# The seam between attention and the MLP: first W1 blocks and x operands asked for during the last value product

## The chip, the cores and the metric

One core of a Trainium2 chip runs one program. The metric is the device time of one execution in microseconds (us), the median of several runs. The engines have queues of their own: TensorE (PE, with its weight loads PEld), VectorE (DVE), ScalarE (ACT), GpSimd (POOL), and SyncE (SP), which here issues nearly all transfers.

## The reference

One bidirectional encoder layer over 2048 positions of width 1024, in float32. The change touches the seam between its last two parts:

```python
    h = h + _cross_attention(_rms_norm(h, norm_x_g[l]), _rms_norm(mem, norm_mem_g[l]),
                             xa_wq[l], xa_wk[l], xa_wv[l], xa_wo[l])
    h = h + jnp.square(jax.nn.relu(_rms_norm(h, norm_ff_g[l]) @ ff_w1[l])) @ ff_w2[l]
return _rms_norm(h, final_norm_g)
```

Ahead of it stand a mixer (a long convolution beside an mLSTM) and its output projection. `ff_w1` is 1024 x 4096, `ff_w2` 4096 x 1024, `mem` has 256 tokens and four heads.

## The kernel before, in words

Activations are kept transposed, channels on the 128 partitions, in blocks of 128 x 512 (256 KB). Every float32 product is made of three: each operand is split into a high half (a rounding copy on ScalarE, line 1539 or 1569) and a low half (a subtraction on VectorE or GpSimd, line 1540 or 1570), and `mm3` (lines 340 to 342) adds high x high, high x low and low x high into one PSUM bank.

**Attention.** `attention` works through four chunks of 512 positions, c = 0 to 3. Each has eight products for the mixer's output projection, the scores with their softmax (tiles `e`, four of them), and eight value products ct = 0 to 7 (24 matmuls each), into which the output weights have been folded. After each value product `finish` adds the residual into a block of `acc`, squares it and adds to the row sum `ssum` (GpSimd, line 1389); `store` writes the block times the norm's gain to `hg` and, after ct = 3 and 7, four residual blocks to `h2` (line 1490, 1 MB). `stats` turns the row sum into the mean square and stores it (line 1518).

**The MLP.** It treats both products as 2 x 2 blocks and makes each with seven block products instead of eight, with sums and differences of blocks. `tp` is the half of the positions, `g` one of 16 groups of 256 hidden channels. `steps` walks (tp, g, i) with i in `ORDER_UP` = 1, 2, 6, 7, 5, 4, 3; the first two groups go side by side, so steps n = 0 and 1 are i = 1 for g = 0 and 1, steps 2 and 3 are i = 2, steps 4 and 5 are i = 6. Each step is one `ffn_product` of 12 matmuls. Its operands:

- x operand i (`ffn_xload` asks for four blocks, `ffn_x` splits them). Operands 1, 2 and 3 are blocks of `hg`; 5, 6, 7 and 4 are sums that `sums_x` has made on GpSimd and stored in `xs`. Four `sums_x` sets for tp = 0 are written into chunk 2's value products.
- weight operand: `load_w1(g)` asks for four W1 blocks (line 1586), makes two sums on GpSimd (lines 1589 and 1590) and, for g below 4, saves them to DRAM for the second half (`save_w1`, line 1577). `ffn_w1` makes the rest of the sums (lines 1611 and 1615) and splits one into `ah`, `al`.

`ffn_pre` fetches x operands 1, 2 and 6 and the weights of the first four steps during chunk 3's value products. In `ffn` the loop asks for W1 of group n at n = 0 and 1, and for x operands 7, 5, 4, 3 at n = 0, 2, 4, 6. Between the value products and this loop stand the first two products and `stats`.

**What sets the order.** The program is written as if in sequence; a planner with a timeline of its own (`schedule_with_timeline_sim`) then fixes the order of each engine's queue, and may take an instruction ahead of others when its data and its buffers are ready. Tiles of one tag share `bufs` buffers in turn: `wr` (6) holds blocks of x and W1 on arrival and also the last mean `mb`; `w` (12) the W1 blocks, in a pool `wring` opened in `ffn`, after attention's pool is closed; `sm` (4) the blocks of `sums_x`; `act`, `wh`, `wl` operands of products. In the up phase the blocks of `acc` serve as scratch, taken in turn from block 1:

```python
def tmp():
    turns[0] += 1
    return self.acc[:, turns[0] % 8]
```

Of the kernel before, what the change touches and what calls it, by code (L numbers as in the profile page):

```python
# [133 lines left out]
class Prog:  # L134
# [1173 lines left out]
    def attention(self, es):  # L1308
        nc, tc, a = self.nc, self.tc, self.a
# [25 lines left out]
        def gemm(w, i, r, p=None, ks=range(8)):  # L1335
            p = p or self.mm()
            ms = slice(128 * i, 128 * i + 128)
            for k in ks:
                self.mm3(p, w[0][:, k, ms], w[1][:, k, ms], r[0][:, k], r[1][:, k], k == 0, k == 7)
            return p  # L1340
# [32 lines left out]
        for c in range(4):  # L1373
# [7 lines left out]
            def finish(ct, p, ssum):  # L1381
                h = acc[:, ct]
                nc.vector.tensor_tensor(h, p, h, ALU.add)
                if ct == 0:
                    nc.scalar.activation(ssum, h, AF.Square)
                else:
                    sq = A.tile([128, 512], F32, tag="sq", name="sq", bufs=1)
                    nc.scalar.activation(sq, h, AF.Square)  # L1388
                    nc.gpsimd.tensor_tensor(ssum, ssum, sq, ALU.add)  # L1389
# [3 lines left out]
            for ct in range(8):  # L1393
                yield 5.2
                if ct % 2 == 0:
                    w = next(wst)
                else:
                    k = sums.pop(0) if sums else None
                    if k is not None:
                        self.sums_x(A, k, "sm")  # L1400
                if c == 0 and ct == 0:
                    half = [gemm(w, i, y, None, range(4)) for i in range(2)]
                    next(mix)
                    residual(0)
                    residual(1)
                if c == 0 and ct < 2:
                    p = gemm(w, ct, y, half[ct], range(4, 8))
                else:
                    p = gemm(w, ct % 2, y)
                if c > 0 and ct < 2:  # L1410
                    residual(ct)
                if ct == 0 and stats is not None:
                    stats()
                if prev is not None:
                    finish(ct - 1, prev, ssum)
                    self.split_gain(s[0][:, ct - 1], s[1][:, ct - 1], acc[:, ct - 1], gx[:, ct - 1:ct])
                prev = p
# [64 lines left out]
            ssum = A.tile([128, 512], F32, tag="ssum", name="ssum", bufs=2)  # L1482
            prev = None

            def store(ct):
                hg = A.tile([128, 512], F32, tag="hg", name="hg", bufs=2)
                nc.scalar.activation(hg, acc[:, ct], AF.Copy, scale=gf[:, ct:ct + 1])
                nc.scalar.dma_start(out=hgd[c, :, ct], in_=hg)
                if ct % 4 == 3:
                    nc.sync.dma_start(out=h2[c, :, ct - 3:ct + 1], in_=acc[:, ct - 3:ct + 1])  # L1490

            for ct in range(8):
                yield 5.2
                if ct % 2 == 0:
                    w = next(wst) if ct else w
                else:
                    k = sums.pop(0) if sums else None
                    if k is not None:
                        self.sums_x(A, k, "sm")
                if c == 3 and ct in (1, 3, 5):  # L1500
                    self.ffn_pre(ct // 2)
                p = gemm(w, ct, o, half[ct], range(4, 8)) if ct < 2 else gemm(w, ct % 2, o)
                if prev is not None:
                    finish(ct - 1, prev, ssum)
                    store(ct - 1)
                prev = p
            finish(7, prev, ssum)
            store(7)

            def stats(c=c, ssum=ssum):  # L1510
                pr = self.hy()
                nc.tensor.matmul(pr, self.ones, ssum, start=True, stop=True)
                if c < 3:
                    mb = A.tile([128, 512], F32, tag="sq", name="mb", bufs=1)
                else:
                    mb = self.R.tile([128, 512], F32, tag="wr", name="mb", bufs=6)
                nc.vector.tensor_scalar(mb, pr, 1.0 / D, EPS, ALU.mult, ALU.add)
                nc.sync.dma_start(out=msd[c], in_=mb)
                pr = self.hy()
                for t in range(4):  # L1520
                    nc.tensor.matmul(pr[:, t:t + 1], ssum[:, 128 * t:128 * t + 128], self.ones[:, 0:1], start=True, stop=True)
                nc.vector.tensor_scalar(rbp[:, 4 * c:4 * c + 4], pr[:, 0:4], 1.0 / D, EPS, ALU.mult, ALU.add)
                nc.vector.scalar_tensor_tensor(rbp[:, 4 * c:4 * c + 4], rbp[:, 4 * c:4 * c + 4], EPS,
                                               rbp[:, 4 * c:4 * c + 4], ALU.mult, ALU.mult)
        self.first = [self.ffn_product(self.wq.pop(0), 1) for _ in range(2)]
        stats()

    ORDER_UP = (1, 2, 6, 7, 5, 4, 3)
    ORDER_DOWN = (1, 6, 7, 5, 3, 2, 4)
# [13 lines left out]
    def ffn_open(self, es):  # L1543
        es.enter_context(self.tc.tile_pool(name="even", bufs=1, side="right")).tile([128, 120], F32, name="even")
        self.R = es.enter_context(self.tc.tile_pool(name="ring", bufs=1, side="right"))
        self.xt, self.rs = {}, es
        self.W, self.WD = {}, {}

    def ffn_xload(self, tp, i):
        hg = self.dram("hg", (4, 128, 8, 512))  # L1550
# [23 lines left out]
        return self.C.tile([128, 512], F32, tag="w", name="w", bufs=12)  # L1574

    def save_w1(self, g, j, t):
        self.nc.sync.dma_start(out=self.dram("w1s", (4, 4, 128, 512))[g, j], in_=t)

    def load_w1(self, g):
        op = self.nc.gpsimd.tensor_tensor  # L1580
# [62 lines left out]
    def ffn(self):  # L1643
# [2 lines left out]
        groups = [(0, (0, 1))] + [(0, (g,)) for g in range(2, 14)] + [(0, (14, 15)), (1, (0, 1))]  # L1646
        groups += [(1, (g,)) for g in range(2, 16)]
        steps = [(tp, g, i) for tp, gs in groups for i in self.ORDER_UP for g in gs]
        self.C = self.rs.enter_context(tc.tile_pool(name="wring", bufs=1, side="right"))
        prods = [(o, i) for o in range(4) for i in self.ORDER_DOWN]  # L1650
        down = [(n, tp, k) for n in range(len(prods)) for tp in range(2) for k in range(4)]
        aq, bq = {}, {}
# [32 lines left out]
        with tc.tile_pool(name="up", bufs=1) as U:  # L1685
# [24 lines left out]
            xsum = list(range(4, 8))  # L1710
            us, cs = {}, {}
            for n, (tp, g, i) in enumerate(steps):
                if n < 2:
                    self.load_w1(n)
                if n < 8 and n % 2 == 0:
                    j = self.ORDER_UP[n // 2 + 3]
                    self.ffn_x(j, self.ffn_xload(0, j))
                if n + 5 < len(steps) and steps[n + 5][0] and steps[n + 5][1] < 4:
                    self.saved.append(self.ffn_w1_saved(*steps[n + 5][1:]))
                if 4 <= n + 2 < len(steps):  # L1720
                    wq.append(self.ffn_w1(*steps[n + 2]))
                if n + 9 >= len(steps) and n + 5 < len(steps):
                    load_w(0, n + 9 - len(steps))
                if n + 2 >= len(steps):
                    k = n + 2 - len(steps)
                    fetch_b(k)
                    fetch_a(0, k)
                if i == 4 and xsum and g % 2 and 2 < g < 13:
                    self.sums_x(self.T, xsum.pop(0), "wn")
                bank = self.ffn_product(wq.pop(0), i) if n > 1 else self.first[n]  # L1730
                u, c = us.setdefault(g, {}), cs.setdefault(g, {})
                if i == 1:
                    u[1] = tmp()
                    nc.scalar.copy(u[1], bank)
                elif i == 2:
                    c[11] = fin(bank, u[1], tp, g, 1)
                elif i == 6:
                    u[2] = plus(bank, u[1])
                elif i == 7:
                    u[3] = plus(bank, u[2])  # L1740
                elif i == 5:
                    c[22] = fin(bank, u[3], tp, g, 3)
                    u[4] = plus(bank, u[2])
                elif i == 4:
                    c[21] = fin(bank, u[3], tp, g, 2)
                else:
                    c[12] = fin(bank, u[4], tp, g, 0)
                    if n + 1 == len(steps):
                        fetch_a(0, 2)
                        fetch_b(2)  # L1750
                        fetch_a(0, 3)
                    t = [self.stage() for _ in range(4)]
                    op = nc.gpsimd.tensor_tensor
                    op(t[0], c[12], c[11], ALU.subtract)
                    op(t[1], c[22], t[0], ALU.subtract)
                    op(t[2], c[22], c[12], ALU.subtract)
                    op(t[3], c[21], t[1], ALU.subtract)
                    for j, x in zip((5, 6, 7, 4), t):
                        out(tp, g, j, x)
                if g == 15 and tp == 0:  # L1760
                    self.ffn_x(i, self.ffn_xload(1, i))
# [241 lines left out]
```

## Time and profile before

| | before |
|---|---|
| median of 3 runs | 3198.08 us |
| the runs | 3193.67, 3198.08, 3198.31 us |
| the profiled execution | 3195.44 us |
| its span, first to last instruction | 3193.7 us |
| mean granted TensorE clock | 0.978 |
| TensorE busy | 96% of the span |
| VectorE, ScalarE, GpSimd busy | 64%, 47%, 36% |
| memory read and written | 404.15 MB, 202.41 MB |

Times in the trace are microseconds from the start of the span. Chunk 3's value products run to about 1909, the up phase begins there. A line number is that of the kernel before. A row of a timeline has start, length, engine, line, operation, output and inputs, count, and in brackets how long the engine had stood idle before it and for whom.

### The profile page before, as it was taken

How to read it: one execution, taken by the hardware profiler on the slowest of the kernel's cores; microseconds unless marked ns; L12 is line 12 of the kernel's file. 1: busy time of each engine (PE TensorE's matmuls, PEld its weight loads, DVE VectorE, ACT ScalarE, POOL GpSimd, SP SyncE). 2: the span in 40 equal slices, each digit the busy share in tenths (PEclk: the TensorE clock that was granted, in tenths of full speed). 3: DMA queues.
4: the chain of work that ended last, by engine and by line, in shares of the span. 5: the costliest groups of instructions: out<-in, count | busy, mean ns of one | idle time of the engine just before them, and what ended most of it. 6: DMA issues, size and time to landing. Idle time of an engine off the chain costs nothing.

```text
span 3193.7 us, 43601 instructions
## 1 busy us (share of the span) xinstructions
PE 3050.3 (96%) x14473; PEld 2399.5 (75%) x14473; DVE 2056.9 (64%) x3563; ACT 1503.6 (47%) x2873; POOL 1156.5 (36%) x802
## 2 busy tenths in 40 slices
PE   6999999999999977999999998999999999999998
PEld 4655566776668766888887886888888878888876
DVE  7775366444874767877775556566655676655695
ACT  5543366424764344454544445556555443333335
POOL 0122012100121334324151217776566483434483
PEclk9999999999999987999999998999999999999999
DMA  5564767686677987556384538656644474444334
GB/s 184 198 207 163 249 194 209 170 272 193 174 230 209 294 268 236 174 164 214 105 298 143 177 118 280 211 196 202 230 154 156 149 249 153 141 132 150 124 93 168
DMA packets 447673, 609.48 MB, mean 191 GB/s; under 512 B 39118, under 2 KB 249166, under 8 KB 446424
## 3 DMA queue, kind: packets, MB, share of 16 engines
q1 hardware_dynamic: 409268, 548.18, 54.0%
q10 hardware_dynamic: 38180, 58.51, 5.5%
q8 instruction: 115, 1.88, 0.3%
q14 instruction: 110, 0.90, 0.1%
HBM read 404.15 MB, written 202.41 MB: 190 GB/s over the span
## 4 chain that ended last, share of the span: by engine, by line
PE 76%; DMA 9%; DVE 7%; issue 3%; ACT 3%; POOL 1%; SPq 1%; ACTq 0%; DVEq 0%; POOLq 0%
PE mm L340 16%; PE mm L342 16%; PE mm L341 16%; PE hy L342 5%; PE hy L340 5%; PE hy L341 5%; PE hy L177 3%; PE hy L876 1%; PE mm L845 1%; PE hy L918 1%; DVE wl L345 1%; DMA xt<-in_x_t_dram 1%; PE hy L1213 1%; PE hy L1215 1%; DMA wn<-in_xa_wq_t_dram 1%
## 5 line engine op out<-in xcount | busy, mean ns | idle before, releaser
L345 DVE TENSOR_TENSOR wl<-wn,wh 128x512 fp32r<-128x512 f32 (+1 forms) x364 | 284.2, 816 | 118.5 <-ACT wh L345 118.2
L1540 DVE TENSOR_TENSOR bl<-wr,bh 128x512 fp32r<-128x512 f32 x213 | 242.1, 1143 | 126.0 <-ACT bh L1539 124.8
L1539 ACT CAST ah<-w 128x512 fp32r<-128x512 f32 x284 | 176.3, 623 | 304.9 <-PE hy L341 159.5
L345 ACT CAST wh<-wn 128x512 fp32r<-128x512 f32 (+1 forms) x364 | 208.1, 618 | 234.7 <-PE mm L342 55.3
L923 POOL TENSOR_TENSOR b<-b,a 128x512 f32<-128x512 f32 x64 | 87.6, 1369 | 583.2 <-ACT b L921 458.8
L340 PE MATMUL mm<-xh,wh 128*128 128x512 f32 x640 | 271.1, 425 | 4.5 <-ACT xh L500 2.3
L341 PE MATMUL mm<-xl,wh 128*128 128x512 f32 x640 | 258.1, 404 | 0.8 <-DVE xl L502 0.6
L342 PE MATMUL mm<-xh,wl 128*128 128x512 f32 x640 | 258.8, 405 | 0.0
L1539 ACT CAST bh<-wr 128x512 fp32r<-128x512 f32 x232 | 143.6, 621 | 235.2 <-PE mm L342 181.8
L1540 DVE TENSOR_TENSOR al<-w,ah 128x512 fp32r<-128x512 f32 x236 | 218.7, 928 | 53.6 <-ACT ah L1539 53.5
L342 PE MATMUL mm<-bh,al 128*128 128x512 f32 x576 | 225.3, 394 | 6.2 <-DVE al L1540 3.3
L340 PE MATMUL mm<-bh,ah 128*128 128x512 f32 x576 | 227.0, 394 | 1.3 <-DVE acc L1697 1.2
L341 PE MATMUL mm<-bl,ah 128*128 128x512 f32 x576 | 226.0, 392 | 0.0
L341 PE MATMUL mm<-act,wh 128*128 128x512 f32 x512 | 200.5, 393 | 0.2 <-DVE act L345 0.2
L342 PE MATMUL mm<-act,wl 128*128 128x512 f32 x512 | 199.3, 391 | 0.1
L340 PE MATMUL mm<-act,wh 128*128 128x512 f32 x512 | 198.2, 393 | 0.1
L340 PE MATMUL hy<-bh,ah 128*128 128x512 f32 x448 | 175.2, 391 | 0.0
L341 PE MATMUL hy<-bl,ah 128*128 128x512 f32 x448 | 174.6, 390 | 0.0
L342 PE MATMUL hy<-bh,al 128*128 128x512 f32 x448 | 174.4, 390 | 0.0
L1389 POOL TENSOR_TENSOR ssum<-ssum,sq 128x512 f32<-128x512 f32 x56 | 82.2, 1467 | 254.5 <-ACT sq L1388 252.6
L340 PEld LDWEIGHTS mm<-xh,wh 128*128 128x128 f32 x640 | 121.8, 190 | 65.6 <-issue 29.7
L341 PEld LDWEIGHTS mm<-xl,wh 128*128 128x128 f32 x640 | 121.4, 190 | 51.6 <-issue 24.2
(378 smaller groups left out, 8487.2 us busy)
## 6 DMA issues: line engine op xcount, KB each, us to landing
wr<-hc SPq DMA_DIRECT2D x224, 256.0 KB
w<-in_ff_w_dram SPq DMA_DIRECT2D x172, 256.0 KB
hc<-wn SPq DMA_DIRECT2D x128, 256.0 KB
wn<-in_w_in_dram SPq DMA_DIRECT2D x100, 256.0 KB
hc<-q SPq DMA_DIRECT2D x96, 256.0 KB
fs<-a SPq DMA_DIRECT2D x32, 512.0 KB
a<-fs SPq DMA_DIRECT2D x64, 256.0 KB
a<-zs SPq DMA_DIRECT2D x64, 256.0 KB
```

The lines of the kernel that those rows point to most:

```text
L177: b = self.nc.tensor.matmul(*products[-1], start=True, stop=True)
L340: mm(ps, lh, rh, start=start, stop=False)
L341: mm(ps, lh, rl, start=False, stop=False)
L342: mm(ps, ll, rh, start=False, stop=stop)
L345: both = (self.nc.scalar.copy(hi, src), self.nc.vector.tensor_tensor(lo, src, hi.bitcast(F32), ALU.subtract))
L845: nc.tensor.matmul(pp, dm[:, m], t[:, m], start=True, stop=True)
L876: nc.tensor.matmul(pg, em[:, m], y, start=True, stop=True)
L918: nc.tensor.matmul(pp, dm[:, m], t[:, m], start=True, stop=True)
L923: nc.gpsimd.tensor_tensor(xt, xt, hi[:, m], ALU.mult)
L1389: nc.gpsimd.tensor_tensor(ssum, ssum, sq, ALU.add)
L1539: self.nc.scalar.copy(hi, src)
L1540: eng.tensor_tensor(lo, src, hi.bitcast(F32), ALU.subtract)
```

## The change

- The W1 ring `wring` is opened with the ring `wr`, before attention ends, and `load_w1(0)` and `load_w1(1)` are called at ct = 4 and 6 of chunk 3's value products, instead of n = 0 and 1 of the up phase.
- x operand 7 is asked for at ct = 6 and split after the last value product; operand 5 is asked for after the first two up products, ahead of `stats`. Operands 4 and 3 move from n = 4 and 6 to n = 2 and 4.
- The last residual store (four blocks of chunk 3) and the store of its mean move to n = 2, behind the loads of operand 4.
- `save_w1` only lists its store; from n = 3 on, each step issues one from the list.
- `sums_x` in attention uses the softmax's tiles `e` instead of four tiles `sm` of its own.

The diff, cut to its core:

```diff
-                        self.sums_x(A, k, "sm")
+                        self.sums_x(A, k, "e")
...
+            def keep(ct, c=c):
+                nc.sync.dma_start(out=h2[c, :, ct - 3:ct + 1], in_=acc[:, ct - 3:ct + 1])
...
-                if ct % 4 == 3:
-                    nc.sync.dma_start(out=h2[c, :, ct - 3:ct + 1], in_=acc[:, ct - 3:ct + 1])
+                if ct == 3 or (ct == 7 and c < 3):
+                    keep(ct)
...
+                if c == 3 and ct in (4, 6):
+                    self.load_w1(ct // 2 - 2)
+                if c == 3 and ct == 6:
+                    x7 = self.ffn_xload(0, 7)
...
+            if c == 3:
+                self.ffn_x(7, x7)
             finish(7, prev, ssum)
             store(7)
...
-                nc.sync.dma_start(out=msd[c], in_=mb)
+                if c < 3:
+                    nc.sync.dma_start(out=msd[c], in_=mb)
+                else:
+                    self.mean = mb
...
         self.first = [self.ffn_product(self.wq.pop(0), 1) for _ in range(2)]
+        self.early_x = self.ffn_xload(0, self.ORDER_UP[4])
         stats()
+
+        def kept():
+            keep(7)
+            nc.sync.dma_start(out=msd[3], in_=self.mean)
+        self.kept = kept
...
         self.R = es.enter_context(self.tc.tile_pool(name="ring", bufs=1, side="right"))
+        self.C = es.enter_context(self.tc.tile_pool(name="wring", bufs=1, side="right"))
...
     def save_w1(self, g, j, t):
-        self.nc.sync.dma_start(out=self.dram("w1s", (4, 4, 128, 512))[g, j], in_=t)
+        self.saves.append(lambda: self.nc.sync.dma_start(out=self.dram("w1s", (4, 4, 128, 512))[g, j], in_=t))
...
-                if n < 2:
-                    self.load_w1(n)
-                if n < 8 and n % 2 == 0:
-                    j = self.ORDER_UP[n // 2 + 3]
-                    self.ffn_x(j, self.ffn_xload(0, j))
+                if n < 6 and n % 2 == 0:
+                    j = self.ORDER_UP[n // 2 + 4]
+                    self.ffn_x(j, self.ffn_xload(0, j) if n else self.early_x)
+                if n == 2:
+                    self.kept()
+                if n > 2 and self.saves:
+                    self.saves.pop(0)()
```

More of the change, by code (lines that the diff above doesn't have):

```diff
@@ L1498, in attention @@
                     if k is not None:
-                        self.sums_x(A, k, "sm")
+                        self.sums_x(A, k, "e")
                 if c == 3 and ct in (1, 3, 5):
                     self.ffn_pre(ct // 2)
+                if c == 3 and ct in (4, 6):
+                    self.load_w1(ct // 2 - 2)
+                if c == 3 and ct == 6:
+                    x7 = self.ffn_xload(0, 7)
                 p = gemm(w, ct, o, half[ct], range(4, 8)) if ct < 2 else gemm(w, ct % 2, o)
@@ L1545, in ffn_open @@
         self.R = es.enter_context(self.tc.tile_pool(name="ring", bufs=1, side="right"))
+        self.C = es.enter_context(self.tc.tile_pool(name="wring", bufs=1, side="right"))
         self.xt, self.rs = {}, es
-        self.W, self.WD = {}, {}
+        self.W, self.WD, self.saves = {}, {}, []
     def ffn_xload(self, tp, i):
@@ L1648, in ffn @@
         steps = [(tp, g, i) for tp, gs in groups for i in self.ORDER_UP for g in gs]
-        self.C = self.rs.enter_context(tc.tile_pool(name="wring", bufs=1, side="right"))
         prods = [(o, i) for o in range(4) for i in self.ORDER_DOWN]
```

## The prediction

> **What bounds the kernel now.** I read the page first, then its stretches around the change, then the instructions of each queue in the worst stretch.
>
> ```profile
> span 3193.7 us, 43601 instructions
> PE 3050.3 (96%) x14473; PEld 2399.5 (75%) x14473; DVE 2056.9 (64%) x3563; ACT 1503.6 (47%) x2873; POOL 1156.5 (36%) x802
> ```
>
> TensorE is busy for 96% of the span, so the change can win only what lies in the other 4%, and what TensorE runs at a lower clock. The table of stretches tells where that is around the change (columns: length; busy time and instructions of PE, PEld, DVE, ACT, POOL; granted clock; DMA share; GB/s).
>
> ```profile
> core 0: us, PE busy (x) PEld busy (x) DVE busy (x) ACT busy (x) POOL busy (x), PEclk, DMA share, GB/s
> 1640.00:1660.00 20.00, 19.91 (x89) 16.15 (x88) 16.17 (x14) 9.55 (x16) 14.78 (x9) 1.00 1.04 354
> 1660.00:1690.00 30.00, 24.40 (x100) 19.40 (x98) 20.93 (x32) 11.30 (x20) 17.11 (x12) 0.89 0.71 236
> 1690.00:1735.00 45.00, 45.00 (x219) 37.70 (x218) 25.33 (x62) 20.06 (x52) 0.00 (x0) 1.00 0.37 117
> 1735.00:1780.00 45.00, 44.83 (x208) 36.56 (x207) 22.23 (x34) 24.21 (x42) 9.10 (x7) 1.00 0.66 224
> 1870.00:1909.00 39.00, 39.00 (x176) 32.02 (x175) 17.78 (x27) 15.95 (x28) 9.43 (x8) 1.00 0.37 129
> 1909.00:1922.00 13.00, 12.93 (x60) 10.13 (x58) 3.04 (x7) 4.92 (x8) 2.58 (x2) 1.00 0.77 248
> 1922.00:1946.00 24.00, 12.57 (x28) 8.48 (x29) 14.87 (x13) 10.78 (x20) 19.93 (x14) 0.57 1.03 345
> 1946.00:1956.00 10.00, 10.00 (x46) 8.26 (x45) 10.00 (x11) 4.64 (x9) 5.91 (x4) 1.00 0.77 237
> 1956.00:2100.00 144.00, 144.00 (x637) 119.25 (x636) 85.85 (x109) 77.32 (x126) 110.48 (x76) 1.00 0.67 222
> ```
>
> A matmul costs 144.00 / 637 = 0.226 us when nothing is late, a product of 12 matmuls 2.7 us. By that price two stretches lose time. From 1922 to 1946, 28 matmuls are worth 6.3 us and took 24.0: **17.7 us lost**, 11.4 idle and the rest at a clock of 0.57. From 1660 to 1690, 100 matmuls are worth 22.6 and took 30.0: **7.4 us lost**. The DMA engines are full where the first hole is (1.03), and two thirds idle just before it (0.37 from 1870 to 1909). TensorE's own rows:
>
> ```profile
> 1921.55 0.39 PE L342 MATMUL hy<-x,al 128*128 128x512 f32 x1
> 1929.53 0.80 PE L340 MATMUL hy<-x,ah 128*128 128x512 f32 x1 [7.60 <-ACT ah L1539]
> 1932.69 0.79 PE L342 MATMUL hy<-x,al 128*128 128x512 f32 x1 [1.94 <-DVE al L1540]
> 1933.71 0.63 PE L341 MATMUL hy<-x,ah 128*128 128x512 f32 x1
> 1934.14 0.63 PE L342 MATMUL hy<-x,al 128*128 128x512 f32 x1
> 1938.42 0.80 PE L340 MATMUL hy<-x,ah 128*128 128x512 f32 x1 [1.09 <-ACT ah L1539]
> 1941.36 0.79 PE L342 MATMUL hy<-x,al 128*128 128x512 f32 x1 [0.87 <-DVE al L1540]
> 1945.74 0.39 PE L340 MATMUL mm<-xh,ah 128*128 128x512 f32 x1
> ```
>
> The fourth product of the up phase ends near 1921.8. The fifth (i=6) waits 7.60 us for ScalarE's half of its weights, and three smaller waits follow. Matmuls start 0.43 us apart here (1933.71, 1934.14) instead of 0.23. Who made the weights late stands in SyncE's queue and its waits:
>
> ```profile
> 1909.99 0.32 SPq L1490 DMA_DIRECT2D h<-acc  x1
> 1910.40 1.36 SPq L1534 DMA_DIRECT2D wr<-xs  x2
> 1916.30 0.32 SPq L1518 DMA_DIRECT2D msd<-mb  x1
> 1916.86 2.11 SPq L1586 DMA_DIRECT2D w<-in_ff_w_dram  x4
> 1919.01 3.55 SPq L1534 DMA_DIRECT2D wr<-xs  x6
> ...
> SPq L1490 <- DVE acc L1383: 17.0, 2, 16.8
> SPq L1518 <- DVE rbp L1522: 4.7, 1, 4.7
> ```
>
> The queue works in order. The residual store (L1490) stands at its head for 16.8 us until VectorE has finished the last value product; the mean store (L1518) then holds it for 4.7 us. Only behind them come the first W1 blocks (L1586, 1916.86) and six blocks of x (L1534, 1919.01). The consumers:
>
> ```profile
> 1922.78 1.26 POOL L1589 TENSOR_TENSOR w<-w 128x512 f32<-128x512 f32 x1 [3.75 <-DMA w<-in_ff_w_dram]
> 1925.46 1.26 POOL L1611 TENSOR_TENSOR w<-w 128x512 f32<-128x512 f32 x1
> ...
> 1925.74 0.62 ACT L1569 CAST xh<-wr 128x512 fp32r<-128x512 f32 x1 [2.42 <-DMA wr<-xs]
> 1928.87 0.61 ACT L1539 CAST ah<-w 128x512 fp32r<-128x512 f32 x1
> 1935.28 0.62 ACT L1569 CAST x<-wr 128x512 fp32r<-128x512 f32 x1 [5.28 <-DMA wr<-xs]
> ```
>
> W1 asked for at 1916.86 is summed at 1922.78, turned into the i=6 operand at 1925.46, split at 1928.87, used at 1929.53. ScalarE also stands at operands of x (2.42 and 5.28 us) with the next weight split behind them.
>
> **The change part by part.**
>
> *W1 blocks and sums, moved.* Eight loads of 256 KB, four GpSimd sums and nothing new: they go from behind the two stores into value products 4 and 6 of the last chunk, counted from 0: to about 1887 and 1898, since eight products of 24 matmuls, 5.4 us each, end at 1909. The planner may take them further ahead: from 1690 to 1735 GpSimd did nothing and DMA stood at 0.37. A load took 1922.78 - 1916.86 = 5.9 us in the full stretch, so even at 1898 the last sum is ready before 1909, and the i=6 subtractions and splits need only two operand buffers, which come free when the first two products end (about 1914). The i=6 product can then start at 1921.8. What hides it: DMA at 0.37, GpSimd busy 9.43 us of 39. Without that cover it would cost the 7.60 again.
>
> *x7 and x5, moved.* x7's four loads go into value product 6, its casts behind product 7; x5's loads ahead of the statistics. x7 has its target buffer from the end of value product 5 (1898), x5 only when the value products end (1909); its four casts at 0.6 us are done by 1914, its use is the ninth product (1909 + 8 x 2.7 + 1.7 of statistics = 1932). x4 and x3 are asked for two steps earlier. So every wait of the hole has its cause removed.
>
> *The two stores, later.* They stop heading the queue. In return the residual store stands behind x4's loads, and a new wait appears: the sixth product's sum overwrites the fifth block of the residual buffer, near 1909 + 6 x 2.7 + 1.7 = 1927, and must wait until the store has read it. Behind that VectorE instruction stand the next weight splits, for which TensorE waits. A transfer of this size under load:
>
> ```profile
> 1635.10 8.01 DMA acc<-in_x_t_dram
> ...
> 1670.67 4.89 DMA xs<-sm
> 1676.03 4.28 DMA xs<-sm
> ```
>
> Asked for between 1916 and 1921, with 8.01 us it lands between 1924 and 1929: it costs 0 to 2 us, less a product in hand. I take 0. The W1 saves become one per step of 2.7 us; the ring wants their buffers for block 2, the fifteenth product, and eight saves are out by the twelfth. A block late for that would cost up to the 5.9 of a load; I take 0.
>
> *What is late next.* From 1909 to 1956 the DMA engines moved 13 x 248 + 24 x 345 + 10 x 237 = 13.9 MB. Twelve blocks (3.1 MB) leave for the time before, 10.7 MB stay, and the stretch shrinks from 47.0 to 29.3 us; at 345 GB/s they need 31.1. So 1.8 us stay by bytes; if ScalarE stands once more before an operand of x, 5.28. Between those I take 4 (bounds 0 and 17.7): **13.7 us gained**.
>
> On a gap that stays, the row first: after 7.60 us idle, matmuls kept a 0.43 us distance for 16 us, across three gaps under 2 us. The Trainium skill (TensorE: Matmul & The Clock Gate, What's actually happening) has the array at half clock after an idle window of some 3.4 us, and at full clock after 3.4 us of sustained work. By it, if the 4 us were one gap, 1.7 us of half-clock work would come on top and the sum would be 12.0; the 16 us in the trace, with gaps among them, are longer than that, and no run here shows which part of it the gaps made.
>
> *The sums of x, moved.* Changing their tile tag acts far from the rest. In the kernel before they had four buffers of their own and ran ahead, beside the first products of chunk 2 (rows: the stores of the sums, TensorE's row sum, chunk 2's last transposes, chunk 3's first softmax):
>
> ```profile
> L1306 SPq DMA_DIRECT2D xs<-sm x16: 319/382/1279, 1602.9 to 1687.3; - x16
> 1681.52 1.87 PE L1470 MATMUL hy<-ones,ssum 128*128 128x1 f32 x8 [4.81 <-POOL ssum L1389]
> 1736.40 2.45 PE L1461 MATMUL hy<-ident,e 128*128 128x128 f32 x16
> 1833.34 0.56 ACT L1447 ACTIVATE e<-mm,mx,qr_y 128x256 f32<-128x256 f32 x1 [1.93 <-DVE mx L1444]
> ```
>
> The stall of 4.81 us at 1681.52 is theirs: GpSimd's row sum stood behind them, and SyncE's queue behind their stores (4.89 and 4.28 us in the chain of waits, above). With the softmax's tag they can begin only when chunk 2's last transposes (1736.40 plus 2.45) give those tiles back, and must be done when chunk 3's softmax wants them (1833.34): 95 us for work that took 1602.9 to 1687.3, 85 us. So the 7.4 us of 1660 to 1690 go, and some come back in the new place, where DMA was at 0.66 and the same queues are shared with the weight columns. Bounds: 7.4 gained, or as much lost again (0 net). I take half, **3.7 us gained**.
>
> **Sum.** 13.7 + 3.7 = 17.4. The profiled execution took 3195.44 (span 3193.7 and 1.7 around it); 3178.0 by it. It lies 2.6 below the median of the runs shown, 1.3 below their mean (3196.7); from the mean: **3179**. The case's own range is 3172 (all 25.1 gained) to 3187 (8 of the hole stay, nothing net from the sums).
>
> **The rivals.** *Half of it.* The hole is filled by transfers, and ScalarE still stands before x4 or x3. For it: a share of 1.03 with 345 GB/s. Against it: some of the bytes there are prefetches for the second half that can wait. With 9 us of the hole gone and the 7.4 given back in full, 3196.7 - 9 = 3188. The Trainium skill (DMA: Bandwidth & Descriptors, Specifications) gives some 358 GB/s for one core's memory; the 10.7 MB would take 29.9 us by it, 0.6 too long, close to the row's 345.
>
> *No effect.* The planner orders every queue by its own estimates; it may put the loads behind another waiting store, or the time may return later in the up phase (DMA 0.67 from 1956 on, TensorE without a gap, which speaks against it). 3192 to 3200.
>
> *Slower.* The sums now meet the value product's column loads in SyncE's queue. Each of the four sets has two waits there like the 4.89 and 4.28: 9.2 us. If column loads have no lead, each set stops TensorE for them: 36.7, against 13.7 + 7.4 gained, 15.6 slower: 3212. It decides from a little over 5 us lost per set (21.1 / 4). For it: one set did stop TensorE in the kernel before, and 8.4 MB more (32 blocks) in a stretch that already moved 224 GB/s. Against it: from 1640 to 1660, at 354 GB/s and with these sums under way, TensorE lost 0.1 us.
>
> **How the numbers follow.** Forecast 0.60, half 0.14, no effect 0.07, slower 0.19. About 0.2% (6.4 us) is what a measurement of this kernel tells from no change: faster is under 3191.7, so the first two cases, 0.74; same 0.07; slower 0.19. The range goes from 3168 to 3206: below lies little, above it most of the slower case.
>
> **What would show it.** Right: W1 loads and their GpSimd sums before 1909, no residual store at the head of SyncE's queue there, TensorE without a gap above 2 us from the fourth product on, clock 1.00, and the stall before the row sum of chunk 2 gone. Wrong: a stall of TensorE between chunk 2's value products and chunk 3's scores with the sums' stores ahead of it; VectorE waiting for the residual store in the sixth product; or ScalarE still waiting for x5, x4 or x3.

## The result and the profile after

The changed kernel took 3172.78 us (median of 6 runs, 3166.02 to 3178.03) against 3197.93 (6 runs, 3188.92 to 3200.67): 0.9925 of the time, interval 0.9911 to 0.994, 24 us less by that ratio (the medians differ by 25.2). Forecast were 3179 and 17.4 less; the range was 3168 to 3206.

The page, the stretches, and the rows of SyncE and GpSimd of the changed kernel (in its listing the W1 loads are line 1605, the loads into `wr` 1552, the residual store 1486, the mean store 1543, the W1 saves 1596, the sums of W1 1608 and on):

```profile
span 3176.3 us, 43590 instructions
PE 3039.3 (96%) x14473; PEld 2393.8 (75%) x14473; DVE 2048.0 (64%) x3563; ACT 1503.0 (47%) x2873; POOL 1157.8 (36%) x802
```

```profile
core 0: us, PE busy (x) PEld busy (x) DVE busy (x) ACT busy (x) POOL busy (x), PEclk, DMA share, GB/s
1640.00:1660.00 20.00, 20.00 (x90) 16.57 (x89) 14.92 (x21) 11.01 (x19) 9.81 (x7) 1.00 1.10 373
1660.00:1690.00 30.00, 30.00 (x138) 24.95 (x137) 24.16 (x36) 12.98 (x25) 14.42 (x10) 1.00 0.65 214
1735.00:1780.00 45.00, 43.60 (x191) 34.79 (x191) 20.98 (x27) 19.99 (x35) 24.07 (x18) 1.00 0.92 325
1909.00:1922.00 13.00, 12.52 (x58) 9.89 (x57) 8.20 (x13) 8.48 (x16) 6.91 (x5) 1.00 0.80 279
1922.00:1946.00 24.00, 24.00 (x108) 19.87 (x107) 20.11 (x23) 15.09 (x26) 13.53 (x10) 1.00 0.80 264
1946.00:1956.00 10.00, 10.00 (x46) 8.29 (x45) 4.99 (x7) 5.95 (x10) 7.98 (x7) 1.00 0.75 265
```

```profile
1642.68 4.71 SPq L1605 DMA_DIRECT2D w<-in_ff_w_dram  x4
...
1652.51 3.26 SPq L1605 DMA_DIRECT2D w<-in_ff_w_dram  x4
1655.87 2.06 SPq L1596 DMA_DIRECT2D w1s<-w  x2
...
1901.09 2.02 SPq L1552 DMA_DIRECT2D wr<-xs  x2
1909.24 0.32 SPq L1486 DMA_DIRECT2D h<-acc  x1
1913.24 0.38 SPq L1605 DMA_DIRECT2D w<-in_ff_w_dram  x1
```

```profile
1651.33 1.37 POOL L1608 TENSOR_TENSOR w<-w 128x512 f32<-128x512 f32 x1 [6.74 <-DMA w<-in_ff_w_dram]
```

Both holes are gone: 108 matmuls instead of 28 from 1922 to 1946, 138 instead of 100 from 1660 to 1690, the clock 1.00 in both. But W1 is not asked for at 1887 and 1898, where the program says so, but from 1642.68 on: the planner took it 245 us ahead of that, into the stretch after the mLSTM. Its first sum is made at 1651.33 and its first saves leave at 1655.87. And the last residual store still leaves at 1909.24, as soon as its data is there, though the program asks for it two products later; the planner took that ahead too.

Where the time went can be read from TensorE's row sums, which every version has. In the kernel before, then after:

```profile
1343.78 0.95 PE L1470 MATMUL hy<-ones,ssum 128*128 128x1 f32 x8
...
1825.58 0.95 PE L1470 MATMUL hy<-ones,ssum 128*128 128x1 f32 x8
...
1914.52 1.02 PE L1512 MATMUL hy<-ssum,ones 128*128 128x512 f32 x2
```

```profile
1350.03 0.95 PE L1470 MATMUL hy<-ones,ssum 128*128 128x1 f32 x8
...
1681.19 0.95 PE L1470 MATMUL hy<-ones,ssum 128*128 128x1 f32 x8
...
1824.84 0.95 PE L1470 MATMUL hy<-ones,ssum 128*128 128x1 f32 x8
...
1914.40 1.12 PE L1521 MATMUL hy<-ssum,ones 128*128 128x512 f32 x2 [0.48 <-POOL ssum L1389]
```

Line 1470 is a chunk's row sum, line 1512 (before) or 1521 (after) the last mean. With chunk 2's row sum of the kernel before at 1681.52 (shown in the prediction), the pieces are, in us, those of the experiments worked out alike from the same rows of their traces:

| version | chunk 0's to chunk 2's row sum | to chunk 3's | to the last mean | to the end of the span |
|---|---|---|---|---|
| before | 337.74 | 144.06 | 88.94 | 1279.2 |
| after | 331.16 | 143.65 | 89.56 | 1261.9 |
| e1 | 331.28 | 144.48 | 88.93 | 1259.1 |
| e2 | 330.95 | 142.33 | 88.93 | 1277.7 |
| e3 | 331.05 | 144.16 | 89.29 | 1274.2 |
| e4 | 330.40 | 143.82 | 89.58 | 1259.7 |
| e5 | 337.75 | 142.86 | 88.94 | 1260.1 |
| e6 | 335.62 | 143.41 | 88.94 | 1278.0 |

From before to after: 6.6 won in the first piece (the stall of the sums), 0.4 won and 0.6 lost in the next two, 17.3 won at the hole: 23.7. The spans differ by only 17.4, because this execution of the changed kernel, the slowest of its six, came to the first row sum 6.25 us later (1350.03 against 1343.78); that 17.4 is also the forecast is chance. Over the eight profiles that start lies anywhere from 1343.8 to 1353.1. The three latest are those of the changed kernel, e3 and e4 (1348.9 to 1353.1); with one trace of each version, whether the change has a part in that or it is the runs' scatter is not shown.

### The profile page after: what moved, and what is told of

Read it like the earlier page. It is cut to its first block, busy times and chain, and to the rows that moved or that the text cites. A ratio compares the mean times of both kernels' runs of the same rounds, so it can differ in the third digit from the quotient of the medians.

```text
span 3176.3 us, 43590 instructions
## 1 busy us (share of the span) xinstructions
PE 3039.3 (96%) x14473; PEld 2393.8 (75%) x14473; DVE 2048.0 (64%) x3563; ACT 1503.0 (47%) x2873; POOL 1157.8 (36%) x802
## 4 chain that ended last, share of the span: by engine, by line
PE 79%; DMA 8%; DVE 7%; issue 3%; ACT 2%; POOL 1%; SPq 0%; ACTq 0%; DVEq 0%; POOLq 0%
PE mm L340 17%; PE mm L342 17%; PE mm L341 17%; PE hy L342 5%; PE hy L340 5%; PE hy L341 5%; PE hy L177 3%; PE hy L876 2%; PE mm L845 2%; PE hy L918 1%; DMA xt<-in_x_t_dram 1%; DVE wl L345 1%; PE hy L1213 1%; PE hy L1082 1%; PE hy L1215 1%
## 5 line engine op out<-in xcount | busy, mean ns | idle before, releaser
L323 POOL TENSOR_TENSOR b<-b 128x512 f32<-128x512 f32 x32 | 59.1, 1848 | 275.8 <-DVE P L685 127.8
```

The costliest lines, as they stand in the source:

```text
L323: nc.gpsimd.tensor_tensor(e[1], f, b, ALU.subtract)
```

## The experiments

Since the program's place for W1 did not set its time, the question was what did. Two theories: the one of the prediction (where the loads stand in the program, and the two stores ahead of them in SyncE's queue; below theory B), and memory (theory A). In the kernel before, the W1 ring (24 KB per partition) opens when attention's pool closes. If it lies partly where attention's tiles lie, no W1 block can land before those are done with; the change frees 8 KB of attention by taking the tiles `sm` away.

**e1: only the tag.**

```diff
-                        self.sums_x(A, k, "sm")
+                        self.sums_x(A, k, "e")
```

> The kernel before with one change: the four sums of x in attention use the softmax's tiles instead of four of their own. Theory A (memory): what counts is the 8 KB per partition that this frees; the W1 ring no longer shares memory with attention's tiles, so the planner takes the W1 loads ahead to about 1640 by itself, though they are still asked for in the up loop. Then nearly the whole gain of the change is here: 3172 to 3177, TensorE without a gap over 2 us after 1909, and the stall of 4.81 us before chunk 2's row sum gone. Theory B (the prediction's: where the loads are asked for, and the stores at the head of the queue): only the stall at 1681 goes, 6 to 7 us, and the gap of 7.6 us with the slow clock after it stays: 3190 to 3192.

Measured: 3170.98 us against 3197.21, 0.9916 (0.9903 to 0.9929). This is the whole gain of the change, with W1 still asked for in the up loop, x7 and x5 in their old places, and both stores where they were. Its stretches, its W1 loads and SyncE's waits near the seam:

```profile
1660.00:1690.00 30.00, 30.00 (x138) 24.96 (x137) 22.98 (x40) 13.05 (x28) 10.81 (x7) 1.00 0.56 168
1922.00:1946.00 24.00, 24.00 (x108) 19.89 (x107) 22.30 (x26) 17.03 (x31) 18.86 (x13) 1.00 0.94 310
```

```profile
1638.47 4.88 SPq L1586 DMA_DIRECT2D w<-in_ff_w_dram  x4
```

```profile
SPq L1490 <- DVE acc L1383: 15.6, 2, 15.3
SPq L1518 <- DVE rbp L1523: 1.6, 1, 1.6
```

W1 goes out at 1638.47. The residual store stands at the head of the queue for 15.3 us, nearly the 16.8 of the kernel before, and TensorE loses nothing: nothing behind it is wanted soon. Theory A holds, theory B falls. With one line edited it is as fast as the whole change, and no version tried was faster than both by more than its interval.

**e2: the tag, with the memory taken up again.** e1 and, in attention, an unused tile that is given back only after the last value product:

```diff
+        pad = A.tile([128, 2048], F32, name="pad")
+        nc.gpsimd.memset(pad[:, 0:8], 0.0)
...
             store(7)
+            if c == 3:
+                nc.gpsimd.tensor_tensor(pad[:, 0:8], pad[:, 0:8], acc[:, 7, 0:8], ALU.add)
```

> As e1, but attention holds an unused tile of 8 KB until the last value product is done, so that the W1 ring's memory is not free earlier than in the kernel before. Theory A: the hole after 1922 is back in full (17 to 18 us lost, gap of 7 to 8 us), only the stall at 1681 is gone: 3190 to 3193. Theory B: the same as e1, whatever that is, since nothing that it names differs between the two. A third reading, that moving the sums costs as much in its new place as it saved, would give 3196 to 3200 here.

Measured: 3191.45 against 3197.21, 0.9984 (0.9975 to 0.9994).

```profile
1910.67 2.11 SPq L1590 DMA_DIRECT2D w<-in_ff_w_dram  x4
```

```profile
1923.28 0.80 PE L340 MATMUL hy<-x,ah 128*128 128x512 f32 x1 [7.59 <-ACT ah L1543]
```

```profile
1915.76:1939.76 24.00, 12.95 (x35) 8.95 (x36) 14.33 (x13) 11.73 (x21) 21.05 (x14) 0.72 1.02 348
```

In this trace the last mean stands at 1908.28, 6.24 us earlier than in the kernel before, and the stretch shown is moved by as much. On the old scale W1 goes out at 1916.9, where it was 1916.86. The gap is back, 7.59 us; the last piece is 1277.7, only 1.5 short of before. The first piece keeps its gain (330.95). So the two gains are separate, and the hole's hangs on the memory.

**e3: all the rest of the change, with the memory taken up.** The changed kernel with e2's tile, the ring opened in `ffn` and W1 asked for in the up loop:

```diff
-                if c == 3 and ct in (4, 6):
-                    self.load_w1(ct // 2 - 2)
...
-        self.C = es.enter_context(self.tc.tile_pool(name="wring", bufs=1, side="right"))
...
+        self.C = self.rs.enter_context(tc.tile_pool(name="wring", bufs=1, side="right"))
...
+                if n < 2:
+                    self.load_w1(n)
```

> The changed kernel with the W1 ring opened in the up phase again, W1 asked for in the up loop, and the unused 8 KB tile held as in e2: x operands early and the two stores late as in the change, W1 late as before. Theory A: W1 is asked for only after the last value product, behind one residual store, at about 1911 instead of 1917, so about 5 to 6 of the 17.7 us are won and a gap of 2 to 4 us stays: 3180 to 3187. Theory B (the two stores at the queue's head made the hole): the hole closes but for 2 us: 3172 to 3177.

Measured: 3187.2 against 3197.21, 0.9966 (0.9953 to 0.9979), at the upper edge of theory A's numbers.

```profile
1912.72 0.32 SPq L1488 DMA_DIRECT2D h<-acc  x1
...
1920.06 2.03 SPq L1606 DMA_DIRECT2D w<-in_ff_w_dram  x4
...
1923.43 0.37 SPq L1545 DMA_DIRECT2D msd<-mb  x1
```

```profile
SPq L1606 <- DMA hg<-hg: 5.4, 1, 5.4
```

```profile
1917.60 1.12 PE L1523 MATMUL hy<-ssum,ones 128*128 128x512 f32 x2 [0.19 <-POOL ssum L1391]
...
1934.41 0.79 PE L340 MATMUL hy<-x,ah 128*128 128x512 f32 x1 [9.31 <-ACT ah L1559]
```

The rows of SyncE decide against the stores. Here the mean store (line 1545) leaves after W1, at 1923.43, and W1 (line 1606) is no earlier: 1920.06 in a run whose last mean stands 3.1 us later (1917.60 against 1914.52), so 1917.0 on the old scale, where it was 1916.86. It stands 5.4 us at the queue's head, and the profile puts that down to the store of attention's last scaled block, the last reader of one of attention's tiles. The gap is 9.31, not the 2 to 4 expected: theory A's own numbers for e3 had W1 out at about 1911, and left this store out.

In the kernel before, the chain of what released what (start, length, what) says the same:

```profile
1909.27 0.70 DVE acc L1383
...
1910.59 0.72 ACT hg L1487
1911.34 5.33 DMA hg<-hg
1916.86 0.38 SPq L1586
```

The last scaled block is stored until 1916.67, and W1 goes out 0.2 us behind that. The store stands in ScalarE's queue and the W1 load reads nothing that it writes, so what can tie them is the memory that the store reads from. The mean store, issued at 1916.30 for 0.32 us, left the queue's head at nearly the same moment. Without it W1 could have gone 0.2 us sooner at most. One thing stays open: the megabyte of the residual store, issued at 1909.99, shared the DMA engines with this store, and since it left ahead of W1 in every version, whether the block would have been stored sooner without it is not shown.

What e3 wins beyond e2 (4.2 us by the medians, 3.5 in the last piece) is not an earlier W1. It may be x7 and x5 being there; the intervals of e2 and e3 touch (0.9975 and 0.9979), so it is hardly clear of the noise.

**e4: the stores asked for in their old places**, everything else as in the change:

```diff
-                if ct == 3 or (ct == 7 and c < 3):
+                if ct % 4 == 3:
                     keep(ct)
...
-                if n == 2:
-                    self.kept()
```

> The changed kernel with the last residual store and the mean store asked for where they were before. Theory A: no difference from the changed kernel, 3170 to 3176, since the trace after shows the residual store still leaving at 1909.24, as soon as its data is there. Theory B: the stores block the queue again and part of the hole returns: 3178 to 3190.

Measured: 3174.69, 0.9933 (0.9921 to 0.9944), not to be told from the change's 0.9925. From 1922 to 1946 its TensorE is full as well:

```profile
1922.00:1946.00 24.00, 24.00 (x107) 19.87 (x107) 19.24 (x24) 14.85 (x26) 13.64 (x9) 1.00 0.84 288
```

**e5 and e6: the memory without the sums.** The sums of x stay on `sm`, at their old time, and 6 KB are found elsewhere; e6 is the control, with an unused tile of 6 KB held as in e2:

```diff
-                hg = A.tile([128, 512], F32, tag="hg", name="hg", bufs=2)
+                hg = A.tile([128, 512], F32, tag="hg", name="hg", bufs=1)
...
-            self.xt[i] = [self.halves(x, ("bh", "bl"), 6, eng[k % 2]) for k, x in enumerate(src)]
+            self.xt[i] = [self.halves(x, ("bh", "bl"), 5, eng[k % 2]) for k, x in enumerate(src)]
...
-            bq[s] = self.halves(self.raw(hc[tp, i - 1, 4 * o + k]), ("bh", "bl"), 6, eng)
+            bq[s] = self.halves(self.raw(hc[tp, i - 1, 4 * o + k]), ("bh", "bl"), 5, eng)
```

> The kernel before with the sums of x on their own four tiles, where they were, and 6 KB freed in another way (one tile for the scaled residual instead of two, five instead of six operand tiles in the MLP), so that the W1 ring no longer shares memory with attention: W1 is taken ahead into the same stretch as the sums. Theory A, with the two gains apart from each other: the hole after 1922 closes (17 to 18 us), the stall before chunk 2's row sum stays at 5 to 8 us: 3178 to 3183 by itself, against e6. Rival: the stretch from 1640 to 1690 was already full at a DMA share of 1.04, so 16 more blocks there (8 loads, 8 saves) lengthen the stall by 6 to 12 us: 3186 to 3192.

> The control of e5: the same two tile counts, and an unused tile of 6 KB held in attention, so that W1 stays late. Theory A and the rival alike: the hole is there (gap of 7 to 8 us after the fourth product) and the stall at 1681 too; the time is that of the kernel before, 3194 to 3200, unless the smaller tile counts cost something by themselves, which is then to be taken off e5.

Measured, against 3196.47: e5 3181.08, 0.9949 (0.9934 to 0.9964); e6 3193.18, 0.9992 (0.9981 to 1.0003). Stretches of e5, then TensorE's gaps in e6:

```profile
1660.00:1690.00 30.00, 26.70 (x111) 20.76 (x111) 25.23 (x31) 9.92 (x18) 25.48 (x17) 0.94 0.91 300
1922.00:1946.00 24.00, 24.00 (x108) 19.87 (x107) 21.54 (x25) 16.03 (x30) 17.22 (x11) 1.00 0.93 301
```

```profile
1682.27 1.05 PE L1472 MATMUL hy<-ones,ssum 128*128 128x1 f32 x8 [2.46 <-POOL ssum L1391]
...
1930.06 0.79 PE L340 MATMUL hy<-x,ah 128*128 128x512 f32 x1 [8.02 <-ACT ah L1543]
```

The hole closes in e5 (last piece 1260.1) and stays in e6 (1278.0, gap of 8.02); the smaller tile counts cost nothing that shows. The stall near 1681 stays in e5 as a loss, 337.75 in the first piece as before, though at a GB/s of 300 and spread over several small gaps. Ten loads and eight saves of W1 went out there from 1644 to 1679; they lengthened that piece by 2.1 us against e6, whose own stall is smaller (2.46, 335.62), and not at all against the kernel before, so the rival's 6 to 12 us did not come. By the medians e5 wins 15.4 us against the kernel before and 12.1 against e6; the pieces give 20.3 and 16.3. The two ways of reading differ by less than the 12 us over which the runs of one version scatter.

## Why the prediction was right, and where

**The number: in its range, in part by luck.** The prediction put 13.7 us on the moves and 3.7 on the new tag of the sums. e1 has the tag alone and wins all of it, 26.2 us by the medians. The moves are needed for none of that; whether they would have won anything with the sums left on `sm` was not tried. The two amounts that were held back, 4 us of the hole and half of the 7.4, were not lost, and so the gain came out 6.6 us above the forecast.

**The two holes and their sizes: right.** 17.7 us were reckoned lost after 1922 and 17.3 came back; 7.4 were reckoned lost from 1660 to 1690 and 6.6 came back.

**What makes the hole: half right.** That W1's lateness opens it was right: each version with W1 early has no hole, each with W1 late has a gap of 7.6 to 9.3 us. That the two stores at the queue's head make W1 late was wrong, and with it the step *The two stores, later*. They stood ahead of W1 in the queue, and the trace showed SyncE waiting for them, but their places in the queue held W1 back by 0.2 us at most: its memory was still attention's (the chain above, and in e3 5.4 us of wait of its own, with the mean store behind it). One of the signs named for right did not come either: the residual store still stood at the queue's head in the changed kernel, for 6.1 us, and cost nothing. A wait at the head of a queue hides the wait of the one behind it. The rival *No effect* named the planner as a reason for the change to do nothing; the planner did undo two of the change's moves, the asking place of W1 and the place of the residual store, and the gain came all the same.

**x7 and x5: needless beside an early W1.** In e1 x7 and x5 are asked for as before and the time is the same. Only with W1 late may they and the late stores bring something together, 3.5 to 4.2 us (e3 against e2), hardly clear of the noise; which of them was not tried apart.

**What is late next: mis-sized.** 4 us were to stay of the hole, none did. The sum of bytes left 10.7 MB for the 29.3 us to which the stretch was to shrink. In the changed kernel the 29.3 us from 1909 hold 130 matmuls, nearly the 134 that took 47.0 us before:

```profile
1909.00:1938.30 29.30, 28.82 (x130) 23.39 (x129) 22.80 (x29) 18.20 (x33) 15.62 (x10) 1.00 0.85 287
```

They moved 29.3 x 287 = 8.4 MB. The error lay in the list of what leaves: eight W1 saves (2.1 MB, the first at 1655.87) went ahead with their sums. Ten saves were issued from 1909 to 1956 in the kernel before, two are left in these 29.3 us. So the stretch ran at a share of 0.85 and not at the 1.03 of before; up to 1956 ScalarE still waited 3.4 us for blocks of x and GpSimd 9.0 for one of W1, TensorE for none.

**The sums in their new place: mis-sized.** Half of the 7.4 was to come back; 6.6 were won and next to nothing came back (143.65 and 89.56 against 144.06 and 88.94). The *Slower* rival needed over 5 us per set. The stretch from 1735 to 1780 is indeed as full as it said, 0.92 and 325 GB/s, and TensorE stood 1.4 us in it. So the sums' stores hardly ever made the weight columns late, full as the stretch was.

**The clock.** In the changed kernel no gap was left to slow the clock. The versions that keep one show more of it than the kernel before. In e3, where the gap is the longest, and in e6 behind a second wait:

```profile
1934.41 0.79 PE L340 MATMUL hy<-x,ah 128*128 128x512 f32 x1 [9.31 <-ACT ah L1559]
...
1939.56 0.63 PE L341 MATMUL hy<-x,ah 128*128 128x512 f32 x1
1939.99 0.48 PE L342 MATMUL hy<-x,al 128*128 128x512 f32 x1
1941.70 0.50 PE L340 MATMUL hy<-x,ah 128*128 128x512 f32 x1 [1.23 <-ACT ah L1559]
1942.03 0.40 PE L341 MATMUL hy<-x,ah 128*128 128x512 f32 x1
1942.27 0.45 PE L340 MATMUL mm<-xh,ah 128*128 128x512 f32 x1
```

```profile
1939.49 0.80 PE L340 MATMUL hy<-x,ah 128*128 128x512 f32 x1 [3.15 <-ACT ah L1543]
...
1942.21 0.59 PE L341 MATMUL hy<-x,ah 128*128 128x512 f32 x1
1942.64 0.39 PE L342 MATMUL hy<-x,al 128*128 128x512 f32 x1
1942.87 0.39 PE L340 MATMUL hy<-x,ah 128*128 128x512 f32 x1
```

After 9.31 us idle matmuls start 0.43 us apart or more until 1939.99, 5.6 us, and then come back to 0.24 across a wait of 1.23 us; after 3.15 us idle the distance of 0.43 lasts to 1942.64, 3.2 us. So half rate can end well before the 16 us that the prediction read from the kernel before. That the waits inside those 16 us made them so long fits this but is not shown by itself.

## What to carry to other kernels

Where a planner takes loads ahead by itself, as here, a load's time can be set by when its buffer's memory is free, and its line in the program says little: before moving a load, ask what lay in its memory before, and who gave that back last. Freeing 8 KB in the stage before was worth as much here as the whole change. A wait seen at the head of a queue is no proof that what stands behind it would have gone sooner; look in the chain of releases for what let the one behind go, or hold its memory and see whether it moves.

## What the runs showed that I had not expected

- DMA can carry more than the 345 GB/s of the hole: 373 GB/s from 1640 to 1660 in the changed kernel, at a share of 1.10, with TensorE without a gap. Why is not shown; it is not that the packets were larger, since there 86% of them were under 2 KB, against 60% in the hole of the kernel before.
- The scatter of one version is large beside these differences: the kernel before took 3191.95 to 3204.13 us in 18 runs of one comparison, while the pieces between row sums, among versions that should agree in them, lie within 1 to 3 us of each other (330.4 to 331.3, 1259.1 to 1261.9). Small differences are read better from pieces than from spans.
